# Indexer's query projection: the order of high and low products in every second weight unit

## The chip, the cores and the metric

The kernel runs on one core of a Trainium2 chip. The metric is the device time of one execution in microseconds; a program is run several times and the median stands for it. The engines named here are TensorE (PE; its weight loads are shown as PEld), VectorE (DVE), ScalarE (ACT), GpSimd (POOL) and SyncE (SP). Each has a queue of its own that it works off in order; they tell each other of finished work by semaphores. DMA engines move data between device memory and the on-chip memory.

## The reference, cut to what matters

The reference is a decoder trunk of two layers over 256 tokens of width 2048. Each layer normalises its input, multiplies it with one wide weight matrix `w_in`, feeds the parts of the product to three token mixers, and merges them. Mixer A picks for each query the 64 keys with the highest score of a small "indexer". The change touches the projection that makes the indexer's queries `qi`: 16 heads of 128 columns each, out of the 2048 input features.

```python
h = rms_norm(x, norm_w)
proj = h @ w_in
(qa, ka, va, za, qi, ki, wi, ...) = jnp.split(proj, split_points(), axis=-1)
...
qi = apply_rope(qi.reshape(b, s, IDX_HEADS, IDX_DIM), cos, sin)
ki = apply_rope(ki.reshape(b, s, 1, IDX_DIM), cos, sin)[:, :, 0]
...
rel = jnp.einsum('bthd,bsd->bhts', qi[:, start:end], ki[:, :end])
score = jnp.einsum('bhts,bth->bts', jax.nn.relu(rel), wi[:, start:end])
_, idx = lax.top_k(score, kk)
```

Since 64 keys are kept, the first 64 queries keep all that they can see, and the kernel computes no indexer query for them: it needs 192 of the 256 tokens.

## The kernel before, in words

**Precision by parts.** TensorE works in a shortened float format (fp32r). A float32 matrix is therefore split in two: a high part, which is a cast, and a low part, which is the float32 value less the high part. A product of two matrices is then three products: high by high, low by high and high by low; the product of the two low parts is left out. For the activations the parts lie ready in the tiles `hx` (helpers `hi` and `part`). For weights they are made as the weights come in.

**Weight units.** Weights come in "units" (`unit`, `load_unit`, `high`, `low`). A unit here is 2 blocks of 128 input features by 512 columns, 512 KB. `load_unit` (L214) issues its transfer from SP's queue into a buffer `raw`, of which there are four. `high` (L225) casts it on ScalarE into `wh`; `low` (L229) takes the difference on VectorE into `wl`. There are three buffers of `wh` and three of `wl`. So a transfer waits until a buffer `raw` is free, which the difference of the unit four before it decides. A cast waits for the transfer and for a free `wh`, which TensorE's last product with the `wh` of the unit three before decides. A difference waits for the cast and for a free `wl`. TensorE waits for the parts of the unit that it multiplies. Each product goes through `mult` (L239), which issues a weight load and a matmul.

**The projection.** The loop `for h in range(0, NIH, 4)` (from L755) runs over four groups of four heads, that is 512 columns. Within a group, `for k0 in range(0, KD, 2)` runs over the 8 units. Each unit has two kinds of product:

- Wide: the activations are the loaded operand and 512 columns of `wh` stream past. Per block of features there are three: the high and the low activations of tokens 128 to 255 into `acc[:, 0]`, and `hq`, which holds the high and the low parts of tokens 64 to 127 side by side, into `acc[:, 1]`. That makes 6 per unit; the trace calls them `acc<-wh,s 128*128 128x512`.
- Narrow: 128 columns of `wl` are the loaded operand and the high activations of 192 tokens stream past. There is one for each of 4 heads and 2 blocks, 8 per unit, into `low_`, a tile of the pool `mm`; the trace calls them `mm<-s,wl 128*128 128x192`.

The wide products come out by token and the narrow ones by feature. Behind a group, ScalarE copies `low_` away into `e` (L776), and `turned` has VectorE transpose `acc` in blocks (L267), GpSimd's queue write it out to device memory (L270) and read it back in the other order (L276) into `zy`. About ten units later `use_i` (L737 to L749, with a `split` at L383 and L384) adds `e` and `zy` and does the rotary turn on VectorE and ScalarE. The rest of such a helper runs when its due time, counted in units, has come; `background` looks for that at the end of each unit.

**What sets the order.** In this stage no order is written out by hand for any engine. A planner puts each engine's instructions in order from the order of the program, from priorities (`tc.high_priority` for loads, casts, differences and transposes) and from edges such as `tc.issue_after`. `hold[0]` keeps the taps of the convolution off VectorE while the stage runs. Before the stage come projections of the convolution branch; behind it come the indexer's key (`chunk_T` with `O_KI`), then the values.

```python
for h in range(0, NIH, 4):
    acc = acc_tile()
    low_ = mm_tile().rearrange("p (f t) -> p f t", f=4)[:, :, :S - TOPK]
    for k0 in range(0, KD, 2):
        wh, wl = unit(w, k0, 2, [(O_QI + h * P, 512)])
        ...
        background(mm)
    e = t4()[:, :4 * (S - TOPK)].rearrange("p (k t) -> p k t", k=4)
    with tc.high_priority():
        nc.scalar.copy(e, low_)
    turned([acc[:, 0, :], acc[:, 1, :]], partial(use_i, h, e), LATER + 1)
```

Of the kernel before, what the change touches and what calls it, by code (L numbers as in the profile page):

```python
# [14 lines left out]
P = 128  # L15
S = 256
NT = S // P
D = 2048
KD = D // P
# [5 lines left out]
TOPK = 64  # L25
# [23 lines left out]
def trunk(ctx: ExitStack, tc: tile.TileContext, x, w_in, xt, w_a, w_b, w_c, w_out,  # L49
# [41 lines left out]
    def slot(dt=F32):  # L91
        return sp.tile([P, KC, S], dt, tag="s8", bufs=12, name=nm("s8"))
# [7 lines left out]
    def parts(n, own=()):  # L100
        own = list(own)
        return own + [slot(F32R).rearrange("p (k w) t -> p k w t", w=2) for _ in range(n // 4 - len(own))]

    def part(b, i, k, n=1, ts=slice(0, S)):
        return b[k // 4][:, k % 4:k % 4 + n, i, ts]

    def hi(b, k, n=1, ts=slice(0, S)):
        return part(b, 0, k, n, ts)
# [7 lines left out]
    def mm_tile():  # L116
        return mp.tile([P, 1024], F32, tag="mm", name=nm("mm"))

    def acc_tile():
        return ap.tile([P, 2, 512], F32, tag="acc", name=nm("acc"))  # L120

    def t4():
        return tp.tile([P, 1024], F32, tag="t4", bufs=4, name=nm("t4"))
# [36 lines left out]
    def background(mm):  # L160
        while pending and pending[0][0] <= count[0]:
            step_on(pending[0])
        for e in stages[:2]:
            if e[1] <= count[0]:
                with tc.issue_after(mm.ins):
                    advance(e)
                break
# [64 lines left out]
    def unit(*args, **kw):  # L232
        u = load_unit(*args, **kw)
        high(u)
        low(u)
        return u[1:]

    def mult(o, lhsT, rhs, start, stop):
        newest[0] = nc.tensor.matmul(o, lhsT, rhs, start=start, stop=stop, skip_group_check=True)  # L239
        return newest[0]  # L240
# [37 lines left out]
    def turned(srcs, use, later=LATER, tmp=None):  # L278


        n = len(srcs)
        if tmp is None:
            tmp = tp.tile([P, n * 512], F32, tag="zt", bufs=1, name=nm("zt"))
        z = away([v.rearrange("p (k e) -> p k e", k=4) for v in srcs], tmp)

        def rest():
            y = tp.tile([P, n * 4, 4, 32], F32, tag="zy", bufs=1, name=nm("zy"))
            back(z, y)
            yield later - 2
            yield from use(y)  # L290

        pending.append([count[0] + 2, rest()])
# [185 lines left out]
    for layer in range(DEPTH):  # L478
# [5 lines left out]
        hx = parts(KD)  # L484
# [267 lines left out]
        hq = slot(F32R).rearrange("p a (b t) -> p (a b) t", t=P)  # L752
        for v in range(KD // 4):
            nc.scalar.copy(hq[:, v * 4:v * 4 + 4, :].rearrange("p k (w t) -> p k w t", w=2), hx[v][:, :, :, TOPK:P])
        for h in range(0, NIH, 4):  # L755


            acc = acc_tile()
            low_ = mm_tile().rearrange("p (f t) -> p f t", f=4)[:, :, :S - TOPK]
            for k0 in range(0, KD, 2):  # L760
                wh, wl = unit(w, k0, 2, [(O_QI + h * P, 512)])
                for k in range(2):
                    kk = k0 + k
                    for i in range(2):
                        mult(acc[:, 0, :], part(hx, i, kk, 1, slice(P, S))[:, 0, :], wh[:, k, :], kk + i == 0,
                             kk == KD - 1 and i == 1)
                    mult(acc[:, 1, :], hq[:, kk, :], wh[:, k, :], kk == 0, kk == KD - 1)
                for k in range(2):
                    kk = k0 + k
                    for f in range(4):  # L770
                        mm = mult(low_[:, f, :], wl[:, k, f * P:(f + 1) * P], hi(hx, kk)[:, 0, TOPK:],
                                  kk == 0 and f % 2 == 0, kk == KD - 1)
                background(mm)
            e = t4()[:, :4 * (S - TOPK)].rearrange("p (k t) -> p k t", k=4)
            with tc.high_priority():
                nc.scalar.copy(e, low_)  # L776
            turned([acc[:, 0, :], acc[:, 1, :]], partial(use_i, h, e), LATER + 1)
# [386 lines left out]
        for t in range(NT):  # L1164
            acc = acc_tile()[:, 0, :]
# [69 lines left out]
```

## Time and profile before

| what | value |
| --- | --- |
| median of 3 runs | 2025.39 us (2024.93 to 2025.48) |
| profiled execution | 2025.48 us, of which the span from the first to the last instruction is 2023.5 us |
| weights' transfers of `w_in` in units of 512 KB | 555, median 4.4 us from issue to landing |
| the stage in layer 0 | 95 to 166 us of the span |
| the stage in layer 1 | 1099 to 1170 us of the span |
| cast to `wh` (L225), 128x1024 | 1.053 us on ScalarE |
| difference to `wl` (L229), 128x1024 | 1.220 us on VectorE |

A row of groups or of the order in time reads: line of the code, engine, operation, the tiles as out<-in, the shapes, xcount. In the order in time the first number is the start, the second the time from there to the end of the last of the count, both in us; what stands in brackets is idle time of the engine ahead of it and what ended it. Matmuls overlap, so a group's time is longer than the pitch of its members times their number. In the rows of stretches the columns are PE, PEld, DVE, ACT and POOL busy with their counts, then TensorE's granted clock (1.00 is full), the busy share of the DMA engines, and GB/s. A row of waits gives who waited for whom, the sum in us, how often, and the longest. "mm" and "acc" are the pools of the accumulators, and "s" stands for a slot of activations.

### The profile page before, as it was taken

The numbers are of one execution on the slowest core, as the hardware profiler recorded it, in microseconds if no ns is written. First come the engines' busy times: TensorE is split into PE (matmuls) and PEld (weight loads), VectorE is DVE, ScalarE is ACT, GpSimd is POOL, SyncE is SP. The second block draws the span as 40 slices with busy tenths as digits, with TensorE's granted clock in tenths as the row PEclk, the third lists the DMA queues.
The fourth block names the chain that finished last, engine by engine and source line by source line (L and its number), as shares of the span: only waits on it lengthen the run. The fifth ranks groups of instructions, "written<-read, shape, count | busy, mean of one in ns | idle before, by whom it ended". The sixth has DMA issues, their size and how long they took to land.

```text
span 2023.5 us, 25956 instructions
## 1 busy us (share of the span) xinstructions
PE 2014.5 (100%) x9508; PEld 1692.8 (84%) x9508; DVE 1517.5 (75%) x2037; ACT 1045.2 (52%) x1213; POOL 169.4 (8%) x284
## 2 busy tenths in 40 slices
PE   9999999999999999999999999999999999999998
PEld 8889888888888888888888898888888888888887
DVE  8668998888778776555785789888886886756565
ACT  7556555566444454444554564555664445544443
POOL 0111022100010000010110101211000100101000
PEclk9999999999999999999999999999999999999999
DMA  7788588855576577776877976788555766676774
GB/s 265 229 290 245 183 247 280 247 176 167 175 234 197 182 222 234 216 232 215 301 233 235 290 214 207 243 267 244 173 166 180 235 195 191 213 251 213 249 223 152
DMA packets 235345, 450.69 MB, mean 223 GB/s; under 512 B 21073, under 2 KB 38481, under 8 KB 235089
## 3 DMA queue, kind: packets, MB, share of 16 engines
q1 hardware_dynamic: 215248, 389.25, 60.9%
q0 software_dynamic: 18304, 56.64, 8.9%
q10 hardware_dynamic: 1664, 3.15, 0.4%
q8 instruction: 74, 1.21, 0.2%
q14 instruction: 55, 0.44, 0.1%
HBM read 416.46 MB, written 32.51 MB: 222 GB/s over the span
## 4 chain that ended last, share of the span: by engine, by line
PE 100%; DVE 0%; ACT 0%; DVEq 0%; issue 0%
PE acc L239 94%; PE mm L239 3%; PE mm L848 1%; PE mm L922 0%; PE mm L996 0%; PE mm L960 0%; PE mm L891 0%; PE mm L626 0%; PE mm L982 0%; PE mm L894 0%; PE mm L819 0%; PE mm L963 0%; PE mm L998 0%; PE mm L984 0%; PE mm L987 0%; PE mm L1013 0%
## 5 line engine op out<-in xcount | busy, mean ns | idle before, releaser
L239 PE MATMUL acc<-wh,s 128*128 128x512 f32 (+2 forms) x5632 | 1380.4, 387 | 0.0
L239 PEld LDWEIGHTS acc<-wh,s 128*128 128x128 f32 x5632 | 1039.0, 188 | 205.8
L229 DVE TENSOR_TENSOR wl<-raw,wh 128x1024 fp32r<-128x1024 f32 (+1 forms) x727 | 876.5, 1209 | 415.1 <-ACT wh L225 403.7
L225 ACT CAST wh<-raw 128x1024 fp32r<-128x1024 f32 (+1 forms) x726 | 755.8, 1044 | 827.7 <-PE acc L239 631.7
L239 PE MATMUL acc<-wl,s 128*128 128x512 f32 (+2 forms) x2624 | 691.1, 385 | 0.0
L239 PEld LDWEIGHTS acc<-wl,s 128*128 128x128 f32 x2624 | 487.6, 188 | 98.9
L270 POOL DMA_DIRECT2D z<-zt x188 | 109.2, 587 | 1442.8 <-DVE zt L267 1086.7
L445 DVE SCALAR_TENSOR_TENSOR s<-yT,cst,s 128x256 f32<-128x256 f32 x480 | 212.9, 480 | 0.0
L239 PEld LDWEIGHTS mm<-s,wl 128*128 128x128 f32 x512 | 66.9, 191 | 5.0
L239 PE MATMUL mm<-s,wl 128*128 128x192 f32 x512 | 66.0, 271 | 0.0
L276 POOL DMA_DIRECT2D zy<-z x48 | 34.5, 718 | 253.5 <-DMA z<-zt 132.7
L267 DVE STREAM_TRANSPOSE zt<-acc 128x512 f32<-128x512 f32 x64 | 44.7, 707 | 4.6 <-PE acc L239 4.5
L384 DVE TENSOR_TENSOR s<-zy,s 128x1024 fp32r<-128x1024 f32 x20 | 24.4, 1222 | 22.7 <-ACT s L383 22.7
L383 ACT CAST s<-zy 128x1024 fp32r<-128x1024 f32 x20 | 21.0, 1048 | 31.9 <-DMA zy<-z 24.1
L1088 DVE TENSOR_TENSOR ev<-acc,ev 128x512 f32<-128x512 f32 x32 | 22.1, 689 | 15.5 <-PE acc L239 15.5
L1078 ACT ACTIVATE ev<-acc 128x512 f32<-128x512 f32 x48 | 26.6, 591 | 0.1
L270 POOL DMA_DIRECT2D z<-t x36 | 20.4, 573 | 48.7 <-DVE t L267 48.7
L239 PE MATMUL acc<-s,wh 128*128 128x512 f32 x96 | 24.0, 392 | 0.0
L1089 DVE TENSOR_TENSOR s<-s,ev 128x512 f32<-128x512 f32 x32 | 22.0, 687 | 0.1
L1120 DVE TENSOR_TENSOR t<-acc,t 128x512 f32<-128x512 f32 (+1 forms) x18 | 10.6, 627 | 12.3 <-PE acc L239 12.3
L239 PEld LDWEIGHTS acc<-s,wh 128*128 128x128 f32 x96 | 17.3, 189 | 3.0
L903 ACT ACTIVATE t<-t,sm 128x128 f32<-128x128 f32 (+1 forms) x32 | 14.3, 447 | 9.4 <-DVE sm L901 9.4
(222 smaller groups left out, 869.7 us busy)
## 6 DMA issues: line engine op xcount, KB each, us to landing
raw<-in_w_in_dram SPq DMA_DIRECT2D x555, 512.0 KB, 4.4
raw<-in_w_out_dram SPq DMA_DIRECT2D x64, 512.0 KB, 4.9
zy<-z POOLq DMA_DIRECT2D x48, 512.0 KB, 5.5
z<-zt POOLq DMA_DIRECT2D x188, 128.0 KB, 4.5
raw<-in_w_a_dram SPq DMA_DIRECT2D x32, 512.0 KB, 3.7
raw<-in_w_c_dram SPq DMA_DIRECT2D x32, 512.0 KB, 4.6
raw<-in_w_b_dram SPq DMA_DIRECT2D x32, 512.0 KB, 4.9
raw<-in_w_in_dram SPq DMA_DIRECT2D x16, 256.0 KB, 3.2
```

What stands on the lines that cost most here:

```text
L225: newest_parts[0] = nc.scalar.copy(u[1], u[0])
L229: newest_parts[1] = sub = nc.vector.tensor_sub(u[2], u[0], u[1].bitcast(F32))
L239: newest[0] = nc.tensor.matmul(o, lhsT, rhs, start=start, stop=stop, skip_group_check=True)
L267: nc.vector.transpose(tmp[:, t].rearrange("p b k i -> p k b i"), src.rearrange("p k (b c) -> p k b c", b=4, c=32))
L270: nc.gpsimd.dma_start(z[:, :, :, a, :].rearrange("t b c e -> c (t b) e"), tmp[a * 32:(a + 1) * 32].rearrange("c t b k i -> c (t b) (k i)"))
L276: nc.gpsimd.dma_start(y.rearrange("p (t a) k i -> p t (a k i)", a=4), z.rearrange("t b c a e -> (b c) t (a e)"))
L383: nc.scalar.copy(h, src)
L384: nc.vector.tensor_sub(l, src, h.bitcast(F32))
L445: nc.vector.scalar_tensor_tensor(o, yT[:, c, q:q + S], wq, o, op0=ALU.mult, op1=ALU.add)
L1078: nc.scalar.activation(sg[t], g[t], AF.Sigmoid)
L1088: nc.vector.tensor_mul(sg[t], y[t], sg[t])
L1089: nc.vector.tensor_add(dst, dst, sg[t])
```

## The change

The order of the two kinds of product is turned round in every second unit of a group. The units with `k0 // 2` even (the first, third, fifth, seventh) run wide, then narrow, as before. The others run narrow, then wide. The last unit of a group is one of these, so a group now ends with its wide products, and the next begins with wide ones. The products themselves, their operands, and the order within each kind are the same. `mm`, which `background` is given, is now the last product of the unit in either order.

```diff
             for k0 in range(0, KD, 2):
                 wh, wl = unit(w, k0, 2, [(O_QI + h * P, 512)])
-                for k in range(2):
-                    kk = k0 + k
-                    for i in range(2):
-                        mult(acc[:, 0, :], part(hx, i, kk, 1, slice(P, S))[:, 0, :], wh[:, k, :], kk + i == 0,
-                             kk == KD - 1 and i == 1)
-                    mult(acc[:, 1, :], hq[:, kk, :], wh[:, k, :], kk == 0, kk == KD - 1)
-                for k in range(2):
-                    kk = k0 + k
-                    for f in range(4):
-                        mm = mult(low_[:, f, :], wl[:, k, f * P:(f + 1) * P], hi(hx, kk)[:, 0, TOPK:],
-                                  kk == 0 and f % 2 == 0, kk == KD - 1)
+
+                for low_turn in ((False, True), (True, False))[k0 // 2 % 2]:
+                    for kk in range(k0, k0 + 2):
+                        if low_turn:
+                            for f in range(4):
+                                mm = mult(low_[:, f, :], wl[:, kk - k0, f * P:(f + 1) * P], hi(hx, kk)[:, 0, TOPK:],
+                                          kk == 0 and f % 2 == 0, kk == KD - 1)
+                        else:
+                            for i in range(2):
+                                mult(acc[:, 0, :], part(hx, i, kk, 1, slice(P, S))[:, 0, :], wh[:, kk - k0, :],
+                                     kk + i == 0, kk == KD - 1 and i == 1)
+                            mm = mult(acc[:, 1, :], hq[:, kk, :], wh[:, kk - k0, :], kk == 0, kk == KD - 1)
                 background(mm)
```

## The prediction

> **What bounds the kernel now.** I read the page first: the engines' busy time and the chain of work that ended last.
>
> ```profile
> span 2023.5 us, 25956 instructions
> ...
> PE 2014.5 (100%) x9508; PEld 1692.8 (84%) x9508; DVE 1517.5 (75%) x2037; ACT 1045.2 (52%) x1213; POOL 169.4 (8%) x284
> ...
> PE 100%; DVE 0%; ACT 0%; DVEq 0%; issue 0%
> PE acc L239 94%; PE mm L239 3%; PE mm L848 1%; PE mm L922 0%; PE mm L996 0%; PE mm L960 0%; PE mm L891 0%; PE mm L626 0%; PE mm L982 0%; PE mm L894 0%; PE mm L819 0%; PE mm L963 0%; PE mm L998 0%; PE mm L984 0%; PE mm L987 0%; PE mm L1013 0%
> ```
>
> TensorE is the bound everywhere: the chain is products and nothing else. A change pays only by making TensorE's own stream shorter, and costs only where a product must wait. The edited loop is "mm L239" (narrow products) and a part of "acc L239". Next I took the two stretches in which it runs, one per layer, then a long stretch of wide products alone, and, in order of time, some pieces of the chain.
>
> ```profile
> 95.05:166.19 71.14, 71.14 (x444) 63.50 (x443) 53.04 (x59) 40.10 (x42) 12.15 (x20) 1.00 0.88 277
> 1099.50:1170.16 70.66, 70.66 (x439) 63.01 (x438) 52.80 (x59) 39.97 (x42) 12.15 (x20) 1.00 0.88 278
> ```
>
> The columns are PE, PEld, DVE, ACT and POOL busy, the granted clock, the DMA share and GB/s. The reader sees that TensorE has no gap here, at full clock, while the DMA engines are 88% busy.
>
> ```profile
> 104.12 0.87 PE mm L239 x8
> 104.99 1.40 PE acc L239 x6
> 106.38 0.87 PE mm L239 x8
> 107.25 1.40 PE acc L239 x6
> 108.65 0.87 PE mm L239 x8
> ```
>
> ```profile
> 525.57 168.69 PE acc L239 x744
> ```
>
> Each weight unit is one run of 6 wide products (1.40 us) and one of 8 narrow ones (0.87 us). Two units take 108.65 - 104.12 = 4.53 us, so one takes 2.265.
>
> **The gain: turns between forms.** Among their own kind wide products cost 168.69 / 744 = 0.227 us each, so six cost 1.36 and not 1.40. The pitch of narrow ones is that of their weight loads:
>
> ```profile
> 106.22 0.86 PEld L239 LDWEIGHTS mm<-s,wl 128*128 128x128 f32 x7
> 107.00 0.19 PEld L239 LDWEIGHTS acc<-wh,s 128*128 128x128 f32 x1
> ```
>
> From the first of seven loads to the load behind them: (107.00 - 106.22) / 7 = 0.111 us a load, where a product of 192 columns could go faster. Eight cost 0.89 among their own kind and 0.87 with a turn ahead of them, since the first one's weights load under the last wide product. A unit without turns would take 1.36 + 0.89 = 2.25, so one pair of turns (wide to narrow and back) costs 2.265 - 2.25 = 0.014 us (with the thirds kept: 1.360 + 0.891 = 2.251). Now each unit has a pair. After the change the order is wide, narrow | narrow, wide | wide, narrow, so two units share a pair. There are 8 units in a group of four heads, 4 groups and 2 layers, 64 units: 32 pairs go, 32 x 0.014 = **0.45 us gained**. No instruction is added or removed; the number of weight loads, products, casts and transfers stays.
>
> Nothing shows 16 narrow products of 192 columns in a row, so I bound it by the nearest runs.
>
> ```profile
> 201.46 1.43 PE mm L848 x12
> ```
>
> This is twelve products of 256 columns: 0.119 each. If the second eight cost that, they take 0.95 in place of 0.87, and with 0.04 saved on the wide side a merge loses 0.04: 32 x 0.04 = 1.3 us lost. At the other end the second eight keep 0.87 and the wide side still saves 0.04: 1.3 us gained. I take the loads' own pitch, since these are the same tiles and shapes.
>
> The Trainium skill, "TensorE: Matmul & The Clock Gate", section "LDWEIGHTS (loading the stationary operand)", gives a load as its columns over 1.2 GHz. As an estimate from that page, 128 columns take 0.107 us, eight take 0.85, and the gain would be 32 x (0.04 + 0.87 - 0.85) = some 1.9 us; the trace's 0.111 decides for the smaller one.
>
> **The cost: the low parts are wanted sooner.** In every second unit (the 2nd, 4th, ... of the stage; "turned" from here on) the narrow products, which read wl, come first, so wl is wanted 1.40 us sooner and wh 0.87 us later. What hides a late wl today is how far ScalarE (cast to wh, L225) and VectorE (difference to wl, L229) run ahead: three buffers each. I paired casts, differences and runs of products in their order. An ordinary turned unit, the 6th, with its difference and its narrow run:
>
> ```profile
> 100.70 1.23 DVE L229 TENSOR_TENSOR wl<-raw,wh 128x1024 fp32r<-128x1024 f32 x1 [0.96 <-ACT wh L225]
> ```
>
> ```profile
> 106.22 1.03 PE L239 MATMUL mm<-s,wl 128*128 128x192 f32 x8
> ```
>
> Its wl was done at 100.70 + 1.23 = 101.93, 4.3 us ahead of the run, and 4.3 - 1.4 = 2.9 us are left after the change. That covers it with no loss. The cover is thin in four places only, where VectorE does the rotary work of an earlier group (L737 to L749) between two differences. The first, in layer 0:
>
> ```profile
> 140.19 1.22 DVE L229 TENSOR_TENSOR wl<-raw,wh 128x1024 fp32r<-128x1024 f32 x1
> ```
>
> ```profile
> 140.22 1.03 PE L239 MATMUL mm<-s,wl 128*128 128x192 f32 x8
> 141.09 1.56 PE L239 MATMUL acc<-wh,s 128*128 128x512 f32 x6
> 142.49 0.70 PE L239 MATMUL mm<-s,wl 128*128 128x192 f32 x5
> ```
>
> This is the 22nd unit, a turned one. Its wl is done at 140.19 + 1.22 = 141.41, before its narrow run at 142.49; wanted at 141.09, it comes 0.32 late, and a load stands 0.09 ahead of its product (the load at 107.00, its product at 107.09 in the row below). **Stall 0.41 us.**
>
> ```profile
> 107.09 1.56 PE L239 MATMUL acc<-wh,s 128*128 128x512 f32 x6
> ```
>
> The same unit in layer 1 has more cover, but here a second effect of the edit bites. The group's last unit is turned, so its wide products are now the last, and the group's accumulator is complete 0.87 us later. VectorE's transposes of it (L267) stand in its queue ahead of later differences:
>
> ```profile
> 1133.06 1.31 DVE L267 STREAM_TRANSPOSE zt<-acc 128x512 f32<-128x512 f32 x2
> 1134.30 1.18 DVE L229 TENSOR_TENSOR wl<-raw,wh 128x1024 fp32r<-128x1024 f32 x1
> ...
> 1138.50 1.83 DVE L746 TENSOR_TENSOR t<-t,cst 128x768 f32<-128x768 f32 x2 [0.61 <-ACT t L743]
> ...
> 1143.05 3.66 DVE L229 TENSOR_TENSOR wl<-raw,wh 128x1024 fp32r<-128x1024 f32 x3
> ```
>
> ```profile
> 1132.86 1.03 PE L239 MATMUL mm<-s,wl 128*128 128x192 f32 x8
> 1133.73 0.65 PE L239 MATMUL acc<-wh,s 128*128 128x512 f32 x2
> ...
> 1145.06 1.56 PE L239 MATMUL acc<-wh,s 128*128 128x512 f32 x6
> ```
>
> The transposes began 0.20 behind the end of the wide run (1132.86); now that end is 1133.73, so they move by 0.87. VectorE is dense from there to 1144.27 save 0.61 that waits for a copy that itself waits for VectorE, so the whole row moves: wl is done at 1143.05 + 1.22 + 0.87 = 1145.14 against 1145.06 wanted. With the 0.09: **stall 0.17 us.** In layer 0 they do not move:
>
> ```profile
> 129.76 0.41 PE L239 MATMUL acc<-wh,s 128*128 128x512 f32 x1
> ```
>
> ```profile
> 130.21 1.31 DVE L267 STREAM_TRANSPOSE zt<-acc 128x512 f32<-128x512 f32 x2
> ```
>
> The next unit begins at 129.76, and 0.20 behind that VectorE is still busy with other work until 130.21. On ScalarE the copy of the narrow products (L776) may go sooner, which only helps.
>
> The other two places are the last unit (the 32nd) of the stage in each layer:
>
> ```profile
> 161.68 1.22 DVE L229 TENSOR_TENSOR wl<-raw,wh 128x1024 fp32r<-128x1024 f32 x1
> ...
> 1165.60 1.22 DVE L229 TENSOR_TENSOR wl<-raw,wh 128x1024 fp32r<-128x1024 f32 x1
> ```
>
> ```profile
> 163.76 1.56 PE L239 MATMUL acc<-wh,s 128*128 128x512 f32 x6
> ...
> 1167.73 1.56 PE L239 MATMUL acc<-wh,s 128*128 128x512 f32 x6
> ```
>
> The margins are 163.76 - 162.90 = 0.86 and 1167.73 - 1166.82 = 0.91. wh of a turned unit is free 0.87 later, so the cast that waits for it, the difference behind it and the rotary work behind that move by up to 0.87: **0.1 us each** with the load's 0.09, between 0 and 0.2. Cost in sum 0.41 + 0.17 + 0.2 = **0.8 us**, between 0 (the casts and differences may come in a better order) and what the rival below makes of it. A product that waits for wl holds the six wide ones behind it. The Trainium skill, same page, section "Step-by-step: what each phase is for", says that products stay in program order and only weight loads are pulled ahead; by that rule the full lateness is paid, by a freer queue none of it (gain 0.45 alone). No run here shows a product overtaking.
>
> Transfers: raw buffers are freed by the differences, so the weight loads on SP that follow a turned unit's cast go 0.87 later and the two of a pair come 1.4 and 3.1 us apart in place of 2.27. The nearest rows are the waits of this stretch:
>
> ```profile
> ACT wh L225 <- PE acc L239: 17.9, 16, 2.9
> ...
> ACT wh L225 <- DMA raw<-in_w_in_dram: 7.6, 7, 2.4
> ```
>
> ```profile
> raw<-in_w_in_dram SPq DMA_DIRECT2D x28, 512.0 KB, 5.4
> ```
>
> More casts wait for TensorE to free a buffer (16) than for a transfer (7), so most transfers land early. The longest such wait, 2.4, is under the 2.9 left: I cost this at nothing and keep it for the rival. POOL's transfers of the group (L270) start up to 0.87 later with the transposes; their results are wanted some ten units on.
>
> **Sum.** -0.45 + 0.8 = +0.35 us. Against the profiled execution (2025.48 us, span 2023.5, about 2 around it) that gives 2025.8; the median of the three runs, 2025.39, lies 0.09 below it, so I forecast **2025.7 us**: no change. About 0.2% (4 us) is what a measurement of this kernel can tell from no change.
>
> **The rivals.**
> 1. *The gain alone.* The rows that speak against it are the four margins, above all the 0.32 late one; for it, that a stall once paid gives all later units more cover, and that the planner may order VectorE's queue otherwise. 2025.39 - 0.45 = 2024.9.
> 2. *Slower: VectorE and the transfers lose their lead.* The place is the turned units from the 18th on in layer 0, where casts already wait for transfers. With transfers in pairs on DMA engines that are 88% busy, one lands up to 2.4 later again, the 2.9 is spent, and the wait is paid in each turned unit. It decides at a loss of 4.05 + 0.45 = 4.5 us, 0.14 us for each of 32 turned units or 1.1 us at each of the four thin places. With 1.5 us at each thin place it is 2025.39 - 0.45 + 6 = 2030.9. Against it: even the late unit above is only 0.32 late.
> 3. *Narrow runs of sixteen go slower* (0.119): 2025.39 + 1.3 + 0.8 = 2027.5. The 0.111 speaks against it.
> 4. *The order is not changed*, as the planner puts products where it likes: 2025.4. Against it: products of the stage run in the order of the code now.
> 5. *Faster by over 0.2%* needs 4.05 / 32 = 0.127 us for each pair of turns; all that a pair costs is 0.014.
>
> **How the numbers follow.** Forecast 0.58, rival 1 0.17, rival 2 0.15, rival 3 0.05, rival 4 0.02, rival 5 0.03. Same: 0.58 + 0.17 + 0.05 + 0.02 = 0.82; slower 0.15; faster 0.03. The range goes from 2024.3 (2025.39, less the gain's upper end of 1.3, with 0.2 of stalls) to 2028.5 (rival 3 and one more microsecond of stalls); it leaves out rival 2's and 5's times.
>
> **What would show it.** In the profile after: pieces of 16 narrow and 12 wide products in the chain; two units in about 4.52 us in place of 4.53; narrow pitch 0.111 inside the sixteen; a gap of some 0.4 us ahead of the 22nd unit in layer 0 that ends with a difference (wl L229); transposes of a group about 0.2 behind the end of its last unit. The prediction is wrong if the gaps of the stage sum to over 4 us, if casts wait for transfers far longer than the 7.6 us now, or if VectorE's order differs and stages behind this one gain gaps.

## The result, and the profile after

The changed kernel takes 2027.84 us (median of 22 runs, 2027.45 to 2028.84) against 2025.11 us before (22 runs, 2024.69 to 2025.95): 2.73 us more, a ratio of 1.0014 with a 95% interval of 1.0008 to 1.0020. That is a little slower, and inside the 0.2% that was called no change. The profiled execution took 2027.88 us, its span is 2025.9.

The changed kernel's profile, the engines' busy time and the chain of work that ended last:

```profile
span 2025.9 us, 25954 instructions
...
PE 2015.0 (99%) x9508; PEld 1692.6 (84%) x9508; DVE 1519.0 (75%) x2037; ACT 1047.5 (52%) x1213; POOL 170.0 (8%) x284
...
PE 99%; ACT 0%; DVE 0%; issue 0%; DVEq 0%; ACTq 0%
```

TensorE's busy time grew by 0.5 us only and 2.4 us of span have been added, so most of it is waits. The two stretches of the edited stage, from the first narrow product to the first product of the indexer's key (columns: PE, PEld, DVE, ACT, POOL busy, clock, DMA share, GB/s), first before, then after:

```profile
94.89:166.03 71.14, 71.14 (x444) 63.49 (x442) 53.04 (x59) 40.10 (x42) 12.15 (x20) 1.00 0.88 278
1098.86:1170.00 71.14, 71.14 (x444) 63.48 (x442) 53.28 (x59) 40.41 (x42) 12.15 (x20) 1.00 0.88 278
```

```profile
94.49:167.04 72.55, 71.65 (x443) 63.58 (x442) 52.71 (x57) 40.40 (x42) 12.20 (x20) 1.00 0.86 270
1099.85:1172.40 72.55, 71.64 (x443) 63.58 (x442) 52.63 (x57) 40.38 (x42) 12.19 (x20) 1.00 0.85 270
```

The stage grew from 71.14 to 72.55 us in each layer, 1.41 twice, and that is all of the loss (in this execution the kernel's beginning, ahead of the stage, was 0.40 shorter: 94.49 against 94.89). Between the stages and behind the second one the two executions agree within 0.03 us (932.83 and 932.81; 853.53 and 853.50). In the chain of the changed kernel the merged runs (two runs of one kind that now stand side by side; below, each such pair of narrow runs is called a merge) are plain:

```profile
103.69 1.76 PE mm L239 x16
105.45 2.76 PE acc L239 x12
108.21 1.76 PE mm L239 x16
...
139.85 0.87 PE mm L239 x8
140.72 0.03 issue
140.75 1.14 PE mm L239 x8
141.88 2.79 PE acc L239 x12
...
159.99 1.41 PE acc L239 x6
161.40 0.03 ACTq L225
161.43 0.79 ACT wh L225
162.22 0.04 issue
162.26 1.66 PE acc L239 x6
163.92 1.88 PE mm L239 x16
```

Two units take 108.21 - 103.69 = 4.52 us, against 4.53 before. Three places are longer: sixteen narrow products at 139.85 take 0.27 more than 1.76 (the 22nd unit), the wide ones from 159.99 to 163.92 take 3.93 in place of 2.76, so 1.17 more (the 31st unit), and the sixteen behind them 0.12 more (the 32nd). The second layer has the same three. Together that is 1.6 us a layer, less 0.22 gained by 16 merges.

The large one is not a wait for low parts. The chain passes through ScalarE: the wide products of the 31st unit wait for their **cast**. ScalarE in order of time there, before and after:

```profile
155.43 0.83 ACT L742 COPY t<-t 64x768 f32<-64x768 f32 x1 [0.35 <-DVE t L740]
156.27 0.83 ACT L743 COPY t<-t 64x768 f32<-64x768 f32 x1
157.40 1.05 ACT L225 CAST wh<-raw 128x1024 fp32r<-128x1024 f32 x1 [0.30 <-DMA raw<-in_w_in_dram]
160.06 0.62 ACT L383 CAST s<-t 128x512 fp32r<-128x512 f32 x1 [1.61 <-DVE t L749]
```

```profile
156.01 0.83 ACT L742 COPY t<-t 64x768 f32<-64x768 f32 x1 [1.21 <-DVE t L740]
156.85 0.83 ACT L743 COPY t<-t 64x768 f32<-64x768 f32 x1
160.64 0.62 ACT L383 CAST s<-t 128x512 fp32r<-128x512 f32 x1 [2.95 <-DVE t L749]
161.17 3.89 ACT L225 CAST wh<-raw 128x1024 fp32r<-128x1024 f32 x4
```

Before, the 31st unit's cast ran at 157.40, between the rotary copies (L742, L743) and the rotary split (L383). After, it stands behind L383. That one waits 2.95 us for VectorE's rotary work (L749), ScalarE is idle meanwhile, and the cast begins at 161.17. ScalarE's queues before and after show this exchange in both layers. Otherwise the order there differs only at the copy of the narrow products (L776 before, L777 after), which now comes one cast sooner in each group. VectorE's queue differs just by the consequences of the exchange and by one transpose at the stage's end.

### The profile page after: what moved, and what is told of

Read it like the earlier page. It is cut to its first block, busy times and chain, and to the rows that moved or that the text cites. A ratio compares the mean times of both kernels' runs of the same rounds, so it can differ in the third digit from the quotient of the medians.

```text
span 2025.9 us, 25954 instructions
## 1 busy us (share of the span) xinstructions
PE 2015.0 (99%) x9508; PEld 1692.6 (84%) x9508; DVE 1519.0 (75%) x2037; ACT 1047.5 (52%) x1213; POOL 170.0 (8%) x284
## 4 chain that ended last, share of the span: by engine, by line
PE 99%; ACT 0%; DVE 0%; issue 0%; DVEq 0%; ACTq 0%
PE acc L239 93%; PE mm L239 3%; PE mm L849 1%; PE mm L923 0%; PE mm L997 0%; PE mm L961 0%; PE mm L892 0%; PE mm L626 0%; PE mm L983 0%; PE mm L895 0%; PE mm L820 0%; PE mm L964 0%; PE mm L999 0%; PE mm L985 0%; PE mm L988 0%; ACT wh L225 0%
## 5 line engine op out<-in xcount | busy, mean ns | idle before, releaser
L239 PEld LDWEIGHTS mm<-s,wl 128*128 128x128 f32 x512 | 62.3, 191 | 3.0 <-DVE wl L229 0.4
L383 ACT CAST s<-zy 128x1024 fp32r<-128x1024 f32 x20 | 21.0, 1049 | 26.7 <-DMA zy<-z 18.9
```

The costliest lines, as they stand in the source:

```text
L383: nc.scalar.copy(h, src)
```

## The experiments

Two theories were set against each other. **Queue order**: the loss is this one wait; the planner puts the cast behind L383 because the buffer that the cast takes over is freed later. **Cover** (how long a part lies ready before TensorE wants it): all 32 turned units, 16 in each layer, free their buffers later and pair the transfers, and the loss is spread over them. Only the condition of the turn was edited, except in the third. The lines are those of the changed kernel, the units are counted from 1 through the four groups. The sets of runs had medians of 2025.09 and 2025.28 us for the kernel before.

| kernel | stage, layer 0 and 1 | against the kernel before |
| --- | --- | --- |
| before | 71.14, 71.14 | |
| the change | 72.55, 72.55 | +2.73 |
| all but the 28th turned | 71.41, 71.45 | +0.44 |
| the 28th alone | 71.39, 71.39 | +0.54 |
| all turned, split one unit later | 71.65, 71.43 | +0.81 |
| groups one and two | 71.03, 71.03 | -0.10 |
| the 26th and 28th alone | 72.29, 72.25 | +2.02 |
| all but the 26th | 71.65, 71.67 | +0.99 |
| all but the 22nd, 26th, 28th, 32nd | 70.98, 70.98 | -0.36 |

The stages repeat far better than the whole. Each row's come from its one profiled execution, and the two layers agree within 0.04 us in every row but one. The beginning of the kernel alone put the first narrow product anywhere from 94.11 to 94.89 us in these profiles. The 95% intervals of the ratios are about 0.0009 to either side, so apart from the change and the kernel with two turned units none of these rows differs from the kernel before by its interval; I go by the stages.

**All but the 28th unit.**

```diff
-                for low_turn in (...)[k0 // 2 % 2]:
+                for low_turn in (...)[k0 // 2 % 2 and (h, k0) != (12, 6)]:
```

> All turned units stay as in the change but one: the 28th unit of the stage (group four, fourth unit) runs wide first. Queue-order theory: the loss of about 1.3 us per layer is one wait, that of the 31st unit's wide products for their cast, because ScalarE's queue has the copy of the rotary work (L383) ahead of that cast; the queue order goes that way because the 28th unit, whose buffer the cast takes over, frees it 0.87 us later. With the 28th unit unturned the cast is ahead of the copy again, so the time falls by 2 x 1.3 = 2.6 us against the change, less 0.03 us for two merges lost: about 0.1 us over the kernel before (2025.2). Cover theory: the loss comes from all 32 turned units freeing buffers later and from paired transfers; one unit less gives back about 0.1 us, so 2.6 us over the kernel before.

Measured: 2025.53 us, ratio 1.0002 (0.9994 to 1.0011). ScalarE has the old order back:

```profile
157.63 1.05 ACT L225 CAST wh<-raw 128x1024 fp32r<-128x1024 f32 x1
160.57 0.62 ACT L383 CAST s<-t 128x512 fp32r<-128x512 f32 x1 [1.88 <-DVE t L749]
```

One turned unit of the sixteen in each layer gave back 2.3 of 2.7 us. The cover theory, which allowed 0.1, falls. What stays, 0.29 of stage, is the 22nd unit's wait of 0.27 and 0.2 at the 32nd, less 0.21 gained.

**The 28th unit alone.**

```diff
+                for low_turn in (...)[(h, k0) == (12, 6)]:
```

> The kernel before with a single turned unit in each layer, the 28th. Queue-order theory: the copy L383 comes ahead of the 31st unit's cast, and the whole wait is there: some 2 to 2.6 us over the kernel before (1.0 to 1.3 per layer), with 0.03 us gained. Cover theory: one turned unit per layer costs nothing that can be measured, within 0.2 us of the kernel before.

Measured: 2025.63 us, ratio 1.0003 (0.9994 to 1.0011). Here my theory missed: the exchange is there, and costs a quarter of what I expected. ScalarE (the 29th unit's cast, the split, and the 31st unit's cast with two more) and TensorE:

```profile
150.97 1.05 ACT L225 CAST wh<-raw 128x1024 fp32r<-128x1024 f32 x1 [0.31 <-PE acc L239]
...
159.22 0.62 ACT L383 CAST s<-t 128x512 fp32r<-128x512 f32 x1 [2.96 <-DVE t L749]
159.75 2.94 ACT L225 CAST wh<-raw 128x1024 fp32r<-128x1024 f32 x3
```

```profile
159.83 1.03 PE L239 MATMUL mm<-s,wl 128*128 128x192 f32 x8
160.85 1.65 PE L239 MATMUL acc<-wh,s 128*128 128x512 f32 x6
```

The 31st unit's cast ends at 160.80, and TensorE would have wanted it at 160.70; with the tail of that wait the stage is 0.25 longer. Counted from the stage's first narrow product, the cast is 3.1 us later than in the kernel before in layer 0 and 3.4 in layer 1, and its cover there was 3.0 and 3.4. So the exchange alone eats the cover and hardly more. The rest of the change's 1.17 needs something that makes the rotary work itself late.

**All turned, and the split of the second group's rotary work one unit later.**

```diff
             nc.vector.tensor_add(e[:, :, TOPK:], e[:, :, TOPK:], s[:, :, TOPK:])
+            if h == 4: yield 1
             split(*(v[:, h:h + 4, :] for v in qi), e[:, :, TOPK:])
```

> All turned units as in the change; only the last step of the rotary work of the second group (the split, L383 and L384) falls due one unit later, so that the 31st unit's cast stands ahead of the copy in ScalarE's queue. Products, transfers and buffers are those of the change. Queue-order theory: the wait for the cast is gone in both layers, 2.4 to 2.6 us less than the change, about 0.1 to 0.3 us over the kernel before; the rest of the rotary work of later groups also moves by up to one unit, behind the stage, which may cost or give some tenths. Cover theory: nothing changes, 2.7 us over the kernel before, since all 32 units are turned.

Measured: 2025.90 us, ratio 1.0003 (0.9994 to 1.0012). With all products in the order of the change, 1.9 of 2.7 us came back, some tenths less than expected: I had left the 22nd unit's waits out of the sum (0.28 in layer 1, 0.5 in layer 0 of this profile, where casts waited 13.8 us for transfers, against 2.7 in the change's). The 31st unit's cast stands ahead of the split again, the wait for it is gone in both layers, and the time behind the stages is unchanged (853.47 us). ScalarE in layer 0:

```profile
158.41 1.05 ACT L225 CAST wh<-raw 128x1024 fp32r<-128x1024 f32 x1
161.23 0.62 ACT L383 CAST s<-t 128x512 fp32r<-128x512 f32 x1 [1.77 <-DVE t L749]
```

**Groups one and two only.**

```diff
+                for low_turn in (...)[k0 // 2 % 2 and h < 8]:
```

> Only groups one and two of each layer have turned units (16 of the 32 merges), where every difference of a turned unit has at least 1.5 us of cover. Both theories: no wait, and the gain alone, 16 x 0.014 = 0.2 us under the kernel before (2024.9). If the merged turns give nothing, 0.0; if the later transposes of group two cost something, up to 0.3 over.

Measured: 2024.99 us against 2025.09, ratio 0.9999 (0.9990 to 1.0008). The stages in both layers:

```profile
94.61:165.64 71.03, 71.03 (x443) 63.48 (x442) 52.25 (x57) 40.28 (x42) 12.16 (x20) 1.00 0.89 278
1098.48:1169.51 71.03, 71.03 (x444) 63.48 (x442) 53.17 (x59) 40.36 (x42) 12.16 (x20) 1.00 0.88 278
```

Eight merges give 0.11 us in each layer, 0.014 each, with no wait. The gain was sized right, and turning as such costs nothing.

After the second experiment the theory was in two steps: the **26th** unit, turned, frees its buffer `wh` 0.87 us later; the 29th unit's cast takes that buffer, and its difference and the rotary work behind it move by as much; the **28th** puts the 31st unit's cast behind that rotary work.

**The 26th and 28th alone.**

```diff
+                for low_turn in (...)[(h, k0) in ((12, 2), (12, 6))]:
```

> The kernel before with two turned units per layer, the 26th and the 28th. Two-step theory: the 26th, turned, frees its buffer 0.87 us later, which moves the 29th unit's cast, the difference behind it and the rotary work behind that by up to 0.9 us; the 28th, turned, puts the copy at the end of that rotary work ahead of the 31st unit's cast. Alone the 28th cost 0.25 us of stage (71.39 against 71.14); with the 26th it should be 0.25 + 0.9 = about 1.15, a stage of 72.25 to 72.3 and 2.2 us over the kernel before. If the loss needs the load of many turned units (cover theory), it stays near 71.4 and 0.5 us over.

Measured: 2027.30 us, ratio 1.0010 (1.0001 to 1.0019). ScalarE and TensorE:

```profile
152.24 1.05 ACT L225 CAST wh<-raw 128x1024 fp32r<-128x1024 f32 x1 [1.10 <-PE acc L239]
...
160.49 0.62 ACT L383 CAST s<-t 128x512 fp32r<-128x512 f32 x1 [2.96 <-DVE t L749]
161.02 2.94 ACT L225 CAST wh<-raw 128x1024 fp32r<-128x1024 f32 x3
```

```profile
160.18 1.03 PE L239 MATMUL mm<-s,wl 128*128 128x192 f32 x8
162.11 1.21 PE L239 MATMUL acc<-wh,s 128*128 128x512 f32 x4 [0.89 <-ACT wh L225]
```

The stage is 72.29 and 72.25, as worked out. Two turned units a layer reproduce four fifths of the stage's growth. The first step is in the rows too: the 29th unit's cast, which waits for TensorE ("PE acc"), begins 57.76 us behind the stage's first narrow product (152.24 - 94.48), against 56.87 with the 28th alone (150.97 - 94.11), and the split behind the rotary work is as much later, 66.01 against 65.11.

**All but the 26th.**

```diff
+                for low_turn in (...)[k0 // 2 % 2 and (h, k0) != (12, 2)]:
```

> All units of the change turned but the 26th. The copy stays ahead of the 31st unit's cast. Two-step theory: the rotary work of the fourth group is no longer late, so the wait for that cast falls from about 1.2 to about 0.3 us; the 22nd unit's 0.3 and about 0.15 at the 32nd stay: a stage of 71.6 to 71.7, some 1.0 us over the kernel before. If the queue order alone set the price, the stage stays at 72.5 and the time 2.7 us over.

Measured: 2026.27 us, ratio 1.0005 (0.9996 to 1.0013); stages of 71.65 and 71.67. With the exchange still in the queue the wait at the 31st unit shrinks to 0.3, here within the twelve wide products that take 2.76 elsewhere:

```profile
160.18 3.02 PE acc L239 x12
```

All but the 28th had no such wait, the 28th without the 26th has 0.3, both together 1.1 or 1.2: both steps are needed for the large wait.

**The other parity.**

```diff
+                for low_turn in (...)[(k0 // 2 + 1) % 2]:
```

> The other units are turned: first, third, fifth, seventh of each group, so a group begins and ends with narrow products; the number of merges is the same, 0.45 us gained. Now the 21st and 31st units want their difference 1.40 us sooner, and in the kernel before these had 0.56 and 1.72 us (layer 0), 1.67 and 1.78 us (layer 1) of cover: waits of about 0.9 and 0 in layer 0, 0 in layer 1 if nothing else moves, each plus up to 0.9 where a cast comes late. In ScalarE's queue the two copies L742 and L743 come ahead of a cast, which moves the rotary work sooner. Theory that thin places and queue order decide: between 0.2 under and 2 us over the kernel before, by the waits that the trace shows at these units and not at the 22nd or 32nd. Theory that turning as such costs: 2.7 us over, as the change.

Measured: 2033.61 us, ratio 1.0041 (1.0027 to 1.0056), 8.3 us slower, far over what I expected. TensorE and ScalarE in layer 0:

```profile
137.19 1.03 PE L239 MATMUL mm<-s,wl 128*128 128x192 f32 x8
140.29 1.14 PE L239 MATMUL mm<-s,wl 128*128 128x192 f32 x8 [2.07 <-DVE wl L229]
141.27 4.52 PE L239 MATMUL acc<-wh,s 128*128 128x512 f32 x12
```

```profile
132.89 0.83 ACT L742 COPY t<-t 64x768 f32<-64x768 f32 x1 [2.85 <-DVE t L740]
...
134.59 2.00 ACT L225 CAST wh<-raw 128x1024 fp32r<-128x1024 f32 x2
```

The waits are where the theory of thin places put them, at the 21st unit (2.3 us in either layer, counted to the next wide product) and the 31st (1.4 in either), and not at the 22nd or 32nd; but both theories' times are far too low. I had sized the waits from the cover of the kernel before, 0.9 and nothing. But in the queue two casts now stand behind the copies L742 and L743, which wait 2.85 us for VectorE. I took that exchange for a help. The four waits make some 7.4 us; with 1.6 more, told further down, less the 0.45 gained, that is about what was lost.

**Without the four units that lose.**

```diff
+                for low_turn in (...)[k0 // 2 % 2
+                                      and (h, k0) not in ((8, 10), (12, 2), (12, 6), (12, 14))]:
```

> The change without the four turned units that lose: the 22nd, 26th, 28th and 32nd of each layer stay unturned; 12 of 16 merges per layer are left. No waits in the stage: 12 x 0.014 = 0.17 us less per layer, a stage of 70.97, and 0.34 us under the kernel before (2024.75).

Measured: 2024.92 us against 2025.28, ratio 0.9998 (0.9989 to 1.0007).

```profile
94.89:165.87 70.98, 70.98 (x444) 63.53 (x442) 53.15 (x58) 40.33 (x42) 12.16 (x20) 1.00 0.88 277
1098.70:1169.68 70.98, 70.98 (x444) 63.53 (x442) 53.27 (x59) 40.48 (x42) 12.14 (x20) 1.00 0.88 278
```

TensorE has no gap, and the stage is 0.16 shorter in each layer, from 12 merges. This is the best version seen. In the profiles its stages beat both kernels; in whole times it beats the change by 2.9 us, while 0.36 us against the kernel before is less than the interval can tell.

## Why the prediction was right or wrong

- **The forecast.** 2025.7 us against 2027.84, 2.1 us too low. The time lies in the range, and the difference of 0.14% in the band called no change. The direction was right (slightly slower, 0.3 us forecast); the size of the cost was not (2.73 us measured). That the time lies in the range is luck: the range reached so far up, to 2028.5, because of rival 3, whose time of 2027.5 is close to the measured one by a cause that did not occur (next point).
- **The gain**, 0.014 us for each merge: right. Eight merges gave 0.11, twelve 0.16. Two units take 4.52 us, and the narrow pitch in the sixteen stays that of the weight loads, (100.68 - 99.12) / 14 = 0.111 us in the rows below; the rival of slower narrow runs (0.119) is out.

```profile
99.12 1.64 PEld L239 LDWEIGHTS mm<-s,wl 128*128 128x128 f32 x14
100.68 0.30 PEld L239 LDWEIGHTS acc<-wh,s 128*128 128x128 f32 x2
```

- **The first thin place**, the 22nd unit: right in kind, 0.41 and 0.17 forecast, 0.27 and 0.28 measured. Layer 0 had its rotary work a little sooner than in the profile before.
- **The last unit**, the 32nd: 0.1 forecast, 0.12 measured behind the long wait at the 31st, and 0.15 where that wait is gone (all but the 28th, layer 0).
- **The step that failed** is "the cover is thin in four places only", with the sum of 0.8 us built on it. I looked for late *low* parts, at turned units, in the queue orders of the kernel before. The largest wait is for a *cast*, at the 31st unit, which is not turned. It is 1.17 us in each layer, 2.3 of the 3.2 us of waits. The prediction had both ingredients: a turned unit's `wh` is free 0.87 later, and the planner's order might differ. It counted the second only as a chance of less cost ("may come in a better order"), and looked for harm from it in VectorE's order alone. It did not ask what a later buffer may do to ScalarE's order: the cast that takes the buffer now stands behind the split.
- **Rival 2** (transfers in pairs, the lead lost in every turned unit) is not what happened. Waits of casts for transfers fell in layer 0, from 7.6 us before to the first of these rows of the change, and rose a little in layer 1, from 3.2 us to the second; turned units in groups one and two cost nothing:

```profile
ACT wh L225 <- DMA raw<-in_w_in_dram: 2.7, 3, 1.7
...
ACT wh L225 <- DMA raw<-in_w_in_dram: 3.8, 3, 3.1
```

- **The order of products.** The merged products, narrow and wide, all waited behind the late one; no run shows a product that overtakes. The rule of the Trainium skill that the prediction weighed ("TensorE: Matmul & The Clock Gate", "Step-by-step: what each phase is for") agrees with that.
- **A stretch read short.** The prediction's row for layer 1 begins at 1099.50, 0.64 us behind the stage's first narrow product, so its 70.66 is not the whole stage, which is 71.14 in both layers. No term of the sum was built on it.
- **What is not settled**: why the planner prefers the split once the 28th unit is turned. That the later free buffer is the reason is argued from the two kernels that differ in this unit alone and from the order in which they come out; the planner's own times are not in any profile.

## What to carry to other kernels

A reorder on the busiest engine changes when buffers come free, and with that the order in which a planner fills the queues of the others; compare those queues before anything else, since one cast behind one blocked copy cost more than all 32 merges gave. Cover must be read for each operand (cast and difference) at each unit, and in the queue order that the new kernel will have. Small regular gains such as 0.014 us a merge can be kept by leaving out the few units where cover is thin.

## What the runs showed of the hardware

In the kernel with the other parity TensorE idled 2.07 us ahead of the 21st unit in both layers. What came next differed. Stretches of layer 0 behind the wait, which ended at 140.29, and the one of layer 1 behind it, the same columns as above:

```profile
140.29:141.80 1.51, 1.51 (x11) 1.42 (x12) 0.82 (x2) 0.93 (x2) 0.00 (x0) 1.00 0.81 283
141.80:145.21 3.41, 3.41 (x10) 2.64 (x9) 3.15 (x4) 2.63 (x3) 0.00 (x0) 0.50 0.61 181
145.21:150.00 4.79, 4.79 (x31) 4.25 (x30) 2.01 (x2) 2.05 (x2) 0.00 (x0) 1.00 0.96 325
```

```profile
1149.40:1153.00 3.60, 3.51 (x19) 3.07 (x20) 2.65 (x5) 2.93 (x4) 0.00 (x0) 1.00 0.83 277
```

In layer 0 the granted clock fell to 0.50 for 3.41 us, from 1.5 us behind the end of the wait, and the twelve wide products took 4.36 us (141.27 to 145.63) where they take 2.76; in layer 1, behind the same wait, it stayed at 1.00. So equal waits of 2 us cost a further 1.6 us in one layer, and nothing in the other. The Trainium skill, "TensorE: Matmul & The Clock Gate", Part 1, gives half the clock as the state after at least one idle window of about 3.4 us, and says that this window is free-running. The clock of 0.50, its 3.41 us and the two outcomes of equal waits agree with that; that 2.07 us of idle time were enough does not. What decided between the two layers is not shown. In the changed kernel itself the waits were at most 0.9 us and the clock stayed at 1.00.
